# Six expert pairs' outputs go through DRAM and are fetched by token, in place of one-hot products

## The chip, the core and the metric

The kernel runs on one core of a Trainium2 chip. The metric is the device time of one execution in microseconds (us). TensorE (PE) does the matrix products and transposes, VectorE (DVE) and ScalarE (ACT) the elementwise work, GpSimd (POOL) broadcasts, fills and some DMA issues, and SyncE (SP) issues the weight loads.

## What is computed

A trunk of two layers on 256 tokens of 1024 values, fp32. In each layer three kinds of token mixer share one projection, then comes a layer norm, then a mixture of 16 experts of which every token uses two, chosen by a router within one of four groups, and a second layer norm. The part that the change touches:

```python
combine = jnp.einsum('tk,tke->te', top_w, one_hot(top_idx, N_EXPERTS))
out = jnp.zeros_like(t)
for e in range(N_EXPERTS):
    act = jax.nn.silu(t @ w_gate[e]) * (t @ w_up[e])
    out = out + combine[:, e:e + 1] * (act @ w_down[e])
...
h = layer_norm(DN_ALPHA * h + ffn, ln_ffn_g[layer], ln_ffn_b[layer])
```

The gate and up matrices are 1024 x 512 and the down matrix is 512 x 1024 for each expert.

## The kernel before

**Tiles.** Tokens stand in two tiles of 128 rows. Each expert has 64 slots (CAP); the tokens that chose it are gathered into them by one-hot products. A token beyond the 64th of an expert would be handled in a branch (`overflow`, L1400), which the given inputs don't enter. The experts are worked in eight pairs, each pair filling 128 slots.

**One pair p.** Gate: eight k-steps of two products each (one for each expert of the pair, 64 columns of weights to 512). Up: eight more. ACT takes Silu of the gate sums, DVE multiplies by the up sums. `by_slot` transposes the weighted one-hot matrix (two transposes into `sT`; `ws` is each slot's combine weight). `turn` transposes the activation (four transposes `aT`), which ACT copies to `actT`. Down: eight steps of two products into two banks `y`. ACT and DVE scale these by `ws` and split them into a high and a low part, `yt`. `scatter` of pair p then goes back to tokens: eight one-hot products `sc` (two token tiles, two halves of the columns, high and low part), whose sums DVE adds into `z`. It stands one pair later in PE's order, around `turn` of pair p+1, so that PE does not wait for the split. The scatter of pair 6 stands in pair 7's gate steps (`SC_AT`); pair 7's own one is spread over the end of the stage. For pairs 2, 4 and 6 one gather (`gather_two`) serves the pair and the one after it.

**The residual.** `halve` keeps the layer input as two parts. `residual`, called four times among pair 6's up steps (one call for each tile and half of the columns), sums the parts, scales them with the norm's two vectors and adds them to `z`: four DVE operations a call. The vectors come by `lnvec`: a 4 KB load on POOL's queue (L355) and a broadcast on POOL (L356).

**Weights.** Everything is loaded once, in tiles of 512 KB, into a ring of 33 slots (`fp`, NFEED). `more()` issues the next tile on SP's queue (L331). It is called once for each tile that PE has used up, and each tile waits for the use that freed its slot. Some tiles go into spare buffers instead (`more_extra`, L314 and L319, the names `wx`). SP issues in order: a load that waits holds up those behind it.

**Order.** In the expert stage each engine runs its instructions in the order in which the code issues them. A planner (`Order`) sets the order of the mixer stages only.

Of the kernel before, what the change touches and what calls it, by code (L numbers as in the profile page):

```python
# [65 lines left out]
N_P0 = 512  # L66
SCRATCH = 2048
# [168 lines left out]
def trunk_kernel(ctx, tc, x, positions, w_in, gate_up, gate_bias, norm_gain, w_out, ln_mix_g, ln_mix_b,  # L236
# [5 lines left out]
    pp = ctx.enter_context(tc.tile_pool(name="pp", bufs=8, space=bass.MemoryType.PSUM))  # L242
    ctx.enter_context(tc.manual_schedule())
# [160 lines left out]
    pref = cp.tile([P, E], F32, name="pref")  # L404
    nc.gpsimd.iota(pref, pattern=[[-1, E]], base=E, channel_multiplier=0, allow_small_or_imprecise_dtypes=True)
# [7 lines left out]
    rc = cp.tile([P, NT, 16], F32, name="rc")  # L413
    rs = cp.tile([P, NT, 2, 8], F32, name="rs")

    def trig_tables():
# [44 lines left out]
        for i in range(2):  # L461
            dve.tensor_copy(rc[:, :, 8 * i:8 * i + 8], trig4[:, 1])
# [53 lines left out]
    def rope(y, off, nh, t):  # L516
# [4 lines left out]
        dve.tensor_mul(ra, v[:, :, 0:16], rc[:, t, None, :].to_broadcast([P, nh, 16]))  # L521
# [197 lines left out]
    for l in range(DEPTH):  # L719
# [646 lines left out]

        def by_slot(Gw):
# [115 lines left out]
        sb, sts = {}, []  # L1483

# [6 lines left out]

        for p in range(E // 2):
            gu = []
            if p == E // 2 - 1:
                Gw = weights(p)
            for nm in ("g", "u"):
                b_ = bank("gu")
                for k in range(KT):
                    if k % 2 == 0:
                        us = [feed.pop((l, nm, p, k + e)) for e in range(2)]  # L1500
                    for e in range(2):
                        mm(b_[64 * e:64 * e + 64], xs[p](k, e), part(us[e], k % 2), start=k == 0, stop=k == KT - 1)
                        if k % 2 and type(us[e]) is not list:
                            more()
# [144 lines left out]
```

## Time and profile before

| | us |
|---|---|
| median of three runs | 746.43 (746.12 to 746.93) |
| the profiled execution | 745.53 |
| its span in the trace | 743.8 |
| PE busy | 715.8 (96%) |
| DVE busy | 373.4 (50%) |
| ACT busy | 255.0 (34%) |
| POOL busy | 43.4 (6%) |
| mean DMA rate over the span | 327 GB/s |

The span is the time from the first to the last recorded event; 1.7 us of the execution lie around it. A busy share is a mean over stages. The expert stage of layer 0 lies at about 155 to 366 us, that of layer 1 at about 515 to 733 us, and what bounds each is read from the stretch itself. In the timelines a line is a run of like instructions, with its start, its length, and in brackets what ended the idle time ahead of it. A product of fp32 is recorded as two instructions, so that x32 there are 16 products.

### The profile page before, as it was taken

What the parts mean: (1) busy time and instruction counts of PE and PEld (TensorE: products, weight loads), DVE (VectorE), ACT (ScalarE), POOL (GpSimd) and SP (SyncE); (2) the same over time, 40 slices, a digit from 0 to 9 for tenths busy, and PEclk for the clock granted to TensorE, in tenths of its full rate; (3) what the DMA queues carried; (4) which work ended last, traced back from release to release, by engine and by line L of the source; (5) the groups of instructions that cost most, each with busy time, mean ns of one, the idle gap of its engine ahead of it and who ended that gap; (6) DMA issues with size and microseconds to landing.
All of it is one profiled execution on the core that took longest, in us unless ns stands there. A gap on an engine that the chain in (4) does not pass through costs nothing. (4 is left out here: it accounts for less than half of the span.)

```text
span 743.8 us, 11218 instructions
## 1 busy us (share of the span) xinstructions
PE 715.8 (96%) x3941; PEld 419.2 (56%) x3941; DVE 373.4 (50%) x986; ACT 255.0 (34%) x527; POOL 43.4 (6%) x67
## 2 busy tenths in 40 slices
PE   7999999999999999999899999999999999999993
PEld 6897977754533533433388888777435344353331
DVE  5887866632312322561488688666231223336405
ACT  5667655422211201210186665563222111111101
POOL 2000001100000002200130000001000000020002
PEclk9999999999999999999999999999999999999997
DMA  8899836889999999999999654569898999999941
GB/s 299 281 392 408 322 135 214 325 312 371 364 343 410 408 410 408 408 409 400 332 387 351 221 176 143 195 207 360 316 380 334 367 408 409 409 408 408 406 177 56
DMA packets 81519, 243.04 MB, mean 327 GB/s; under 512 B 9956, under 2 KB 14120, under 8 KB 81448
## 3 DMA queue, kind: packets, MB, share of 16 engines
q1 hardware_dynamic: 80776, 241.86, 86.2%
q8 instruction: 36, 0.59, 0.3%
q10 hardware_dynamic: 416, 0.26, 0.1%
q14 instruction: 35, 0.29, 0.1%
q0 software_dynamic: 256, 0.03, 0.0%
HBM read 241.08 MB, written 1.05 MB: 326 GB/s over the span
## 5 line engine op out<-in xcount | busy, mean ns | idle before, releaser
L231 PE MATMUL gu<-wf,xT 128*64 128x512 f32 x944 | 224.3, 593 | 3.0 <-PEq L1400 3.0
L231 PEld LDWEIGHTS gu<-wf,xT 128*64 128x64 f32 x944 | 72.8, 137 | 136.8 <-issue 126.9
L231 DVE TENSOR_TENSOR wlo<-wf,whi 128x512 fp32r<-128x512 f32 (+2 forms) x174 | 97.3, 598 | 39.6 <-ACT whi L231 36.9
L231 PE MATMUL y<-wf,actT 128*64 128x512 f32 x456 | 110.7, 596 | 1.4 <-ACT actT L231 1.4
L231 ACT ACTIVATE whi<-wf 128x512 fp32r<-128x512 f32 (+2 forms) x176 | 86.8, 552 | 14.5 <-PE po L231 9.5
L231 DVE TENSOR_TENSOR act<-act,gu 128x512 f32<-128x512 f32 x16 | 11.0, 687 | 141.9 <-PE gu L231 86.5
L231 PE MATMUL pj<-whi,hhi 128*128 128x512 f32 (+2 forms) x224 | 81.7, 365 | 0.0
L231 PE MATMUL pj<-wlo,hhi 128*128 128x512 f32 (+2 forms) x224 | 78.2, 349 | 1.6 <-DVE wlo L231 1.5
L231 PE MATMUL pj<-whi,hlo 128*128 128x512 f32 (+2 forms) x224 | 77.7, 347 | 0.0
L231 DVE SCALAR_TENSOR_TENSOR yt<-y,ws,yt 128x512 fp32r<-128x512 f32 x32 | 23.8, 750 | 106.6 <-ACT yt L231 105.4
L231 PEld LDWEIGHTS y<-wf,actT 128*64 128x64 f32 x456 | 33.8, 137 | 58.5 <-issue 51.8
L231 ACT ACTIVATE yt<-y,ws 128x512 fp32r<-128x512 f32 x32 | 21.8, 688 | 100.6 <-PE y L231 100.1
L231 PEld LDWEIGHTS pj<-whi,hhi 128*128 128x128 f32 x224 | 42.1, 188 | 8.3 <-issue 2.9
L231 PEld LDWEIGHTS pj<-wlo,hhi 128*128 128x128 f32 x224 | 42.2, 188 | 7.1 <-DVE wlo L231 3.4
L231 PEld LDWEIGHTS pj<-whi,hlo 128*128 128x128 f32 x224 | 42.1, 188 | 5.2
L231 ACT ACTIVATE xT<-xT,cols 128x256 f32<-128x256 f32 (+1 forms) x40 | 18.2, 518 | 72.0 <-PE xT L231 72.0
L231 PE MATMUL sc<-yt,sT 128*128 128x512 f32 x128 | 36.7, 414 | 1.8 <-ACT yt L231 1.7
L231 ACT ACTIVATE act<-gu 128x512 f32<-128x512 f32 x16 | 9.6, 597 | 79.5 <-PE gu L231 67.0
L231 PE MATMUL gu<-wx,xT 128*64 128x512 f32 x80 | 36.6, 592 | 0.0
L231 ACT ACTIVATE actT<-aT 128x512 f32<-128x512 f32 x16 | 9.6, 598 | 70.0 <-PE aT L231 70.0
L231 DVE TENSOR_TENSOR z<-z,sc 128x512 f32<-128x512 f32 x48 | 29.7, 679 | 7.7 <-PE sc L231 7.7
L231 PEld LDWEIGHTS sc<-yt,sT 128*128 128x128 f32 x128 | 21.9, 189 | 12.5 <-issue 4.9
(269 smaller groups left out, 966.1 us busy)
## 6 DMA issues: line engine op xcount, KB each, us to landing
wf<-in_w_expert_up_dram SPq DMA_DIRECT2D x120, 512.0 KB, 9.6
wf<-in_w_expert_gate_dram SPq DMA_DIRECT2D x116, 512.0 KB, 7.6
wf<-in_w_expert_down_dram SPq DMA_DIRECT2D x114, 512.0 KB, 10.1
wf<-in_w_in_dram SPq DMA_DIRECT2D x32, 512.0 KB, 9.8
wf<-in_w_out_dram SPq DMA_DIRECT2D x16, 512.0 KB, 10.3
wx<-in_w_expert_down_dram SPq DMA_DIRECT2D x24, 256.0 KB, 6.0
wf<-in_w_in_dram SPq DMA_DIRECT2D x16, 292.0 KB, 5.9
wf<-in_w_in_dram SPq DMA_DIRECT2D x16, 264.0 KB, 4.9
```

The lines of the kernel that those rows point to most:

```text
L231: return fn(*a, **kw)
```

## The change

Pairs 0 to 5 (N_AWAY = 6) no longer scatter. Their down sums are scaled by `ws` into one tile `yw` (ACT one half, DVE the other), and a DMA on ACT's queue stores its 128 rows, 512 KB, in a DRAM buffer `away` of 768 rows. `yw` takes a slot of the weight ring. `rows_of` works out for each token, in eight small DVE operations, the rows of its two expert outputs in `away`; a row outside of the buffer (an expert of pairs 6 or 7, or a token beyond its expert's slots) is skipped. After pair 5, POOL clears `z` and `zb` (two tiles of 128 x 1024 each) and, at the second gate step of pair 6 in the code, `fetch` issues four indirect DMAs of 128 rows, one row for each token: first choices into `z`, second ones into `zb`. `residual` has one more addition, that of `zb`. `shares` gets `ws` from two products of two columns, where `by_slot` made two transposes. `scatter` remains for pairs 6 and 7.

Where PE's order had scatters ahead of the down products, gate steps of the next pair now stand (FILL: two ahead of `turn` and one behind it, or one behind it where a `gather_two` is there already). `yw` and `zb` take eight slots of the ring in each layer, and for these no `more()` is called. A smaller edit makes the table `rc` of the rotary embedding half as wide.

```diff
+N_AWAY = 6
+FILL = (2, 3)
+FETCH = (6, 1)
...
+            dve.tensor_add(r, zb[t][:, c], r)
             dve.tensor_add(z[t][:, c], z[t][:, c], r)
...
+        def shares(p):
+            b_ = bank("ws")
+            for t in range(NT):
+                mm(b_[:, 0:2], Gs[p][:, t].rearrange("p a b -> p (a b)"), comb[:, t * E + 2 * p:t * E + 2 * p + 2],
+                   start=t == 0, stop=t == NT - 1)
+            ws = sm("ws", 1)
+            for e in range(2):
+                dve.tensor_copy(ws[64 * e:64 * e + 64], b_[64 * e:64 * e + 64, e:e + 1])
+            od.free(b_)
+            return ws
+        def rows_of():
+            code, c2, rows = sm("code", 32), sm("code", 32), sm("rows", 2 * NT, I32)
+            code3, low = code.rearrange("p (t e) -> p t e", t=NT), sm("low", 2 * NT)
+            dve.tensor_scalar(code, pos, float(CAP), 4096.0, op0=OP.is_ge, op1=OP.mult)
+            dve.tensor_add(code, code, pos)
+            dve.tensor_add(code3, code3, first[:, None, :].to_broadcast([P, NT, E]))
+            dve.tensor_reduce(low[:, 0:NT], code3, AX.X, OP.min)
+            c3 = c2.rearrange("p (t e) -> p t e", t=NT)
+            dve.tensor_tensor(c3, code3, low[:, 0:NT, None].to_broadcast([P, NT, E]), op=OP.is_equal)
+            dve.scalar_tensor_tensor(c2, c2, 8192.0, code, op0=OP.mult, op1=OP.add)
+            dve.tensor_reduce(low[:, NT:2 * NT], c3, AX.X, OP.min)
+            dve.tensor_copy(rows, low)
+            return rows
...
         def scatter(p, yt, sT, tiles=range(NT)):
-            if p == 0:
-                z.extend(t4("z", (P, D)) for _ in range(NT))
             for t in tiles:
                 for n in range(2):
                     b_ = bank("sc")
                     place(b_, t, n, yt, sT)
                     zs = z[t][:, 512 * n:512 * n + 512]
-                    if p == 0:
-                        act.activation(zs, b_, AF.Copy)
-                    else:
-                        dve.tensor_add(zs, zs, b_)
+                    dve.tensor_add(zs, zs, b_)
                     od.free(b_)
+        def fetch():
+            for i, zt in enumerate(z + zb):
+                nc.gpsimd.indirect_dma_start(out=zt, out_offset=None, in_=away,
+                                             in_offset=bass.IndirectOffsetOnAxis(ap=rows[:, i:i + 1], axis=0),
+                                             bounds_check=N_AWAY * P - 1, oob_is_err=False)
...
+        rows = rows_of()
+        away = dp.tile([N_AWAY * P, D], F32, name="away", tag=f"away{l}")
+        zb = []
...
+        def step(p, nm, b_, k):
+            if k % 2 == 0:
+                us[nm] = [feed.pop((l, nm, p, k + e)) for e in range(2)]
+            for e in range(2):
+                mm(b_[64 * e:64 * e + 64], xs[p](k, e), part(us[nm][e], k % 2), start=k == 0, stop=k == KT - 1)
+                if k % 2 and type(us[nm][e]) is not list:
+                    more()
+            if (p, nm) == (FIN, "u") and k in BEGIN:
+                begin(*((0, 0), (1, 0), (0, 1))[BEGIN.index(k)])
+            if (p, nm, k) == (FIN, "g", SC_AT):
+                scatter(*late)
+            if (p, nm, k) == (FIN, "g", OVER_AT):
+                overflow()
+            if nm == "g" and (p, k) == FETCH:
+                fetch()
+            if k % 2 and (p, nm) in AT:
+                {"h": halve, "r": residual}[AT[p, nm]](k // 4, k // 2 % 2)
+        def gate(p, upto):
+            if p not in gates:
+                gates[p], done_k[p] = bank("gu"), 0
+            while done_k[p] < upto:
+                step(p, "g", gates[p], done_k[p])
+                done_k[p] += 1
...
+            if p < N_AWAY:
+                ws = shares(p)
+            else:
+                sT, ws = by_slot(Gw)
...
-            elif p + 1 in xs:
-                scatter(*late, (0,))
+            elif p == 0:
+                gather(1, G, turn)
+            else:
+                if p + 1 in TWO:
+                    gather_two(p + 1, G)
+                else:
+                    gate(p + 1, FILL[0])
                 turn()
-                scatter(*late, (1,))
-            elif not late:
-                gather(p + 1, G, turn)
-            else:
-                (gather_two if p + 1 in TWO else gather)(p + 1, G)
-                turn()
-                scatter(*late)
+                gate(p + 1, FILL[1] if p + 1 not in TWO else FILL[1] - FILL[0])
...
+                        elif p < N_AWAY and yw is None:
+                            yw = fp.tile([P, D], F32, name="yw", tag="wf")
+                        elif p == N_AWAY - 1 and len(zb) < NT:
+                            zb.append(fp.tile([P, D], F32, name="zb", tag="wf"))
...
-                    split(py[n], *yt[n], scale=ws)
-                if p == E // 2 - 1:
+                    if p < N_AWAY:
+                        c = slice(512 * n, 512 * n + 512)
+                        if n == 0:
+                            act.activation(yw[:, c], py[n], AF.Copy, scale=ws)
+                        else:
+                            dve.tensor_scalar(yw[:, c], py[n], ws, None, op0=OP.mult)
+                            nc.scalar.dma_start(away[p * P:(p + 1) * P], yw)
+                    else:
+                        yt[n] = [t2("yt", dt=F32R) for _ in range(2)]
+                        split(py[n], *yt[n], scale=ws)
+                if final:
...
+            if p >= N_AWAY:
+                late = p, yt, sT
+            if p == N_AWAY - 1:
+                z.extend(t4("z", (P, D)) for _ in range(NT))
+                for zt in z + zb:
+                    pool.memset(zt, 0.0)
```

**PE, layer 0, from pair 5's `turn` to the scatter of pair 6.** `gu` are gate and up sums, `sc` scatters, `y` down sums, `aT` and `sT` transposes. Before:

```order
L231 MATMUL aT<-ident,act 128x128 x4
L231 MATMUL sc<-yt,sT 128x512 x8
L231 MATMUL y<-wf,actT 64x512 x16
L231 MATMUL gu<-wf,xT 64x512 x32
L231 MATMUL sT<-ident,Gw 128x128 x2
L231 MATMUL sc<-yt,sT 128x512 x4
L231 MATMUL aT<-ident,act 128x128 x4
L231 MATMUL sc<-yt,sT 128x512 x4
L231 MATMUL y<-wf,actT 64x512 x16
L231 MATMUL gu<-wf,xT 64x512 x12
L231 MATMUL sc<-yt,sT 128x512 x8
```

And now:

```order
L234 MATMUL aT<-ident,act 128x128 x4
L234 MATMUL gu<-wf,xT 64x512 x2
L234 MATMUL y<-wf,actT 64x512 x16
L234 MATMUL gu<-wf,xT 64x512 x30
L234 MATMUL sT<-ident,Gw 128x128 x2
L234 MATMUL gu<-wf,xT 64x512 x4
L234 MATMUL aT<-ident,act 128x128 x4
L234 MATMUL gu<-wf,xT 64x512 x2
L234 MATMUL y<-wf,actT 64x512 x16
L234 MATMUL gu<-wf,xT 64x512 x6
L234 MATMUL sc<-yt,sT 128x512 x8
```

The scatters of pairs 4 and 5 are gone; one gate step of pair 6 (x2) and three of pair 7 (x4 and x2) have moved ahead of the down products in their places. The scatter of pair 6 remains.

**POOL, layer 0, from the last vector's broadcast on.** `mc` are constants of the next mixer. Before:

```order
L355 DMA vec<-in_ln_ffn_b_dram 1x16x64
L356 ISA vec<-vec 128x1024
L375 MEMSET mc 128x256
L376 AFFINE_SELECT mc<-mc 128x128
L378 AFFINE_SELECT mc<-ones 128x128
```

And now:

```order
L360 ISA vec<-vec 128x1024
L234 MEMSET z 128x1024 x2
L234 MEMSET zb 128x1024 x2
L1429 DMA z<-away,rows 128x1024 x2
L1429 DMA zb<-away,rows 128x1024 x2
L379 MEMSET mc 128x256
L380 AFFINE_SELECT mc<-mc 128x128
L382 AFFINE_SELECT mc<-ones 128x128
```

Four clears and four fetches stand between the broadcast and the next layer's constants.

**SP, layer 1, from the last loads into spare buffers to the load of a counter `cnti`.** Before:

```order
L314 DMA wx<-in_w_expert_up_dram 128x1024
L314 DMA wx<-in_w_expert_down_dram 128x1024
L314 DMA wx<-in_w_expert_gate_dram 128x1024
L331 DMA wf<-in_w_expert_down_dram 128x1024 x4
L331 DMA wf<-in_w_expert_gate_dram 128x1024 x6
L331 DMA wf<-in_w_expert_up_dram 128x1024 x7
L331 DMA wf<-in_w_expert_down_dram 128x1024 x3
L1580 TENSOR_LOAD cnti
```

And now:

```order
L318 DMA wx<-in_w_expert_up_dram 128x1024
L318 DMA wx<-in_w_expert_down_dram 128x1024
L318 DMA wx<-in_w_expert_gate_dram 128x1024
L335 DMA wf<-in_w_expert_up_dram 128x1024 x7
L335 DMA wf<-in_w_expert_down_dram 128x1024 x5
L335 DMA wf<-in_w_expert_gate_dram 128x1024 x6
L335 DMA wf<-in_w_expert_up_dram 128x1024
L1653 TENSOR_LOAD cnti
```

The tiles that follow the last spare load belong to an earlier place in the weights than before; behind it SP has eight more tiles ahead of any given one.

## Rows read from the trace of the kernel before

**Rows 1.** The page: span, engines, groups (line, operation, tiles, count, busy, mean ns, idle).

```profile
span 743.8 us, 11218 instructions
...
PE 715.8 (96%) x3941; PEld 419.2 (56%) x3941; DVE 373.4 (50%) x986; ACT 255.0 (34%) x527; POOL 43.4 (6%) x67
...
L231 PE MATMUL gu<-wf,xT 128*64 128x512 f32 x944 | 224.3, 593 | 3.0 <-PEq L1400 3.0
...
L231 PE MATMUL y<-wf,actT 128*64 128x512 f32 x456 | 110.7, 596 | 1.4 <-ACT actT L231 1.4
...
L231 ACT ACTIVATE actT<-aT 128x512 f32<-128x512 f32 x16 | 9.6, 598 | 70.0 <-PE aT L231 70.0
```

**Rows 2.** Busy by stretch: length, PE, PEld, DVE, ACT, POOL, clock, DMA share, GB/s.

```profile
155.00:225.00 70.00, 70.00 (x364) 31.14 (x364) 19.03 (x49) 16.29 (x31) 0.00 (x0) 1.00 0.91 345
...
225.00:350.00 125.00, 123.52 (x600) 50.96 (x596) 44.67 (x82) 16.32 (x27) 9.10 (x13) 1.00 1.03 408
...
515.00:600.00 85.00, 83.91 (x442) 38.11 (x442) 25.59 (x79) 19.37 (x35) 0.00 (x0) 1.00 0.94 354
...
600.00:717.00 117.00, 115.48 (x560) 48.08 (x556) 41.17 (x74) 14.94 (x25) 7.32 (x8) 1.00 1.01 400
```

**Rows 3.** Timeline of SP's queue: start, us, issues.

```profile
310.90 9.30 SPq L331 DMA_DIRECT2D wf<-in_w_expert_gate_dram  x8
...
341.61 7.98 SPq L331 DMA_DIRECT2D wf<-in_w_in_dram  x7
...
514.43 0.33 SPq L314 DMA_DIRECT2D wx<-in_w_expert_gate_dram  x1
...
676.55 9.13 SPq L331 DMA_DIRECT2D wf<-in_w_expert_gate_dram  x8
```

**Rows 4.** DMA issues (230 to 320; last: whole span), median us to landing.

```profile
wf<-in_w_expert_gate_dram SPq DMA_DIRECT2D x26, 512.0 KB, 10.2
...
vec<-in_ln_ffn_b_dram POOLq DMA_DIRECT2D x1, 4.0 KB, 5.4
...
out_dram<-z SPq DMA_DIRECT2D x3, 256.0 KB, 2.0
```

**Rows 5.** Timeline of PE, layer 0: pairs 5 to 7, next mixer's first product.

```profile
300.60 2.09 PE L231 MATMUL sc<-yt,sT 128*128 128x512 f32 x8
...
302.62 7.09 PE L231 MATMUL y<-wf,actT 128*64 128x512 f32 x32
...
309.54 13.90 PE L231 MATMUL gu<-wf,xT 128*64 128x512 f32 x64
...
323.37 0.44 PE L231 MATMUL sT<-ident,Gw 128*128 128x128 f32 x2
...
324.58 0.60 PE L231 MATMUL aT<-ident,act 128*128 128x128 f32 x4
...
326.04 7.09 PE L231 MATMUL y<-wf,actT 128*64 128x512 f32 x32
...
372.19 1.15 PE L231 MATMUL pj<-wf,hT 128*128 128x292 f32 x4
```

**Rows 6.** The same of layer 1: pair 6's down products.

```profile
691.12 7.09 PE L231 MATMUL y<-wf,actT 128*64 128x512 f32 x32
```

**Rows 7.** Timeline of POOL: fourth vector's transfer and broadcast, layer 0.

```profile
306.61 0.51 POOL L355 DMA_DIRECT2D vec<-in_ln_ffn_b_dram  x1 [6.11 <-PE y L231]
...
312.13 1.29 POOL L356 PARTITION_BROADCAST vec<-vec  x1 [5.02 <-DMA vec<-in_ln_ffn_b_dram]
```

**Rows 8.** POOL's instructions by line: a clear of 128x1024.

```profile
L231 POOL MEMSET aM<- 128x1024 f32 x2 | 1.9, 958 | 130.3 <-PE pT L231 66.4 <-DVE acc L231 64.0
```

**Rows 9.** Timeline of DVE: last addition of a quarter, product of gate and up.

```profile
317.44 0.69 DVE L231 TENSOR_TENSOR z<-z,whole 128x512 f32<-128x512 f32 x1
...
323.61 0.68 DVE L231 TENSOR_TENSOR act<-act,gu 128x512 f32<-128x512 f32 x1
```

**Rows 10.** Busy by stretch, after PE's last product (columns of Rows 2).

```profile
736.00:744.00 8.00, 0.00 (x0) 0.00 (x0) 4.53 (x5) 0.35 (x1) 2.61 (x2) 0.51 0.35 131
```

More of the change, by code (lines that the diff above doesn't have):

```diff
@@ L403, in trunk_kernel @@
     nc.gpsimd.iota(iota, pattern=[[1, CAP]], base=0, channel_multiplier=0, allow_small_or_imprecise_dtypes=True)
-    pref = cp.tile([P, E], F32, name="pref")
-    nc.gpsimd.iota(pref, pattern=[[-1, E]], base=E, channel_multiplier=0, allow_small_or_imprecise_dtypes=True)
+    pref = cp.tile([P, 4], F32, name="pref")
+    nc.gpsimd.iota(pref, pattern=[[-1, 4]], base=E, channel_multiplier=0, allow_small_or_imprecise_dtypes=True)
+    first = cp.tile([P, E], F32, name="first")
+    nc.gpsimd.iota(first, pattern=[[CAP, E]], base=0, channel_multiplier=0, allow_small_or_imprecise_dtypes=True)
     below = cp.tile([P, 4, 4], I32, name="below")
@@ L460, in trig_tables @@
         trig4 = trig.rearrange("p (s t j) -> p s t j", s=2, t=NT)
-        for i in range(2):
-            dve.tensor_copy(rc[:, :, 8 * i:8 * i + 8], trig4[:, 1])
+        dve.tensor_copy(rc, trig4[:, 1])
         dve.tensor_scalar(rs[:, :, 0], trig4[:, 0], -1.0, None, op0=OP.mult)
@@ L1492, in trunk_kernel @@
+        def gate(p, upto):
[4 more added lines that the diff above has]
+                done_k[p] += 1
         for p in range(E // 2):
-            gu = []
-            if p == E // 2 - 1:
+            final = p == FIN
+            if final:
                 Gw = weights(p)
[L1496 to L1504, printed above, removed]
-                    if (p, nm) == (E // 2 - 1, "u") and k in BEGIN:
-                        begin(*((0, 0), (1, 0), (0, 1))[BEGIN.index(k)])
-                    if (p, nm, k) == (E // 2 - 1, "g", SC_AT):
-                        scatter(*late)
-                    if (p, nm, k) == (E // 2 - 1, "g", OVER_AT):
-                        overflow()
-                    if k % 2 and (p, nm) in AT:
-                        {"h": halve, "r": residual}[AT[p, nm]](k // 4, k // 2 % 2)
-                gu.append(b_)
-                if nm == "g":
-                    av = t2("act")
-                    act.activation(av, b_, AF.Silu)
-                    if p + 1 < E // 2:
-                        Gw = weights(p)
-                        if p + 1 not in Gs:
-                            G = slots(p + 1)
@@ L1521, in trunk_kernel @@
-            dve.tensor_mul(av, av, gu[1])
-            od.free(*gu)
-            sT, ws = by_slot(Gw)
+            gate(p, KT)
+            av = t2("act")
+            act.activation(av, gates[p], AF.Silu)
+            if not final:
+                if p >= N_AWAY:
+                    Gw = weights(p)
+                if p + 1 not in Gs:
+                    G = slots(p + 1)
+            bu = bank("gu")
+            for k in range(KT):
+                step(p, "u", bu, k)
+            dve.tensor_mul(av, av, bu)
@@ L1551, in trunk_kernel @@
             yt = [None, None]
-            us = [feed.pop((l, "d", p, i)) for i in range(8)]
-            final = p == E // 2 - 1
+            ud = [feed.pop((l, "d", p, i)) for i in range(8)]
+            yw = None
             for i in range(8):
```

21 lines of the change are left out of this document (12 added, 9 removed).

## The prediction

> **What bounds the kernel now.** I read the page's head and its costly groups first [rows 1]: TensorE (PE) is busy for 715.8 of 743.8 us, and its two large groups in the expert stage waited for nothing that costs: 3.0 us before gate and up products (that is the overflow branch), 1.4 before down products. By that alone, work taken off PE is time won. Next I read the busy times by stretch [rows 2], since a share over the whole span hides stages. In the first part of each expert stage PE never idles and the DMA engines move 345 and 354 GB/s; in the second part PE is still full, but DMA is full too, at 408 and 400 GB/s. So the stage is bounded twice there. How near the second bound lies is read from SyncE's (SP) weight issues [rows 3] and their time to landing [rows 4] against PE's order [rows 5]. The eight gate tiles of pair 7 are issued from 310.90 on, and a full DMA passes one in 1.28 us (512 KB at 408 GB/s). The second is out at 312.2 and down 10.2 later, at 322.4. PE reads it after pair 6's down products, at 326.04 + 6.9 = 333. Ten us of lead: whatever PE wins beyond that, or DMA gets to carry beside it, is a wait for weights.
>
> **What comes off PE.** Each scatter is eight products, 2.02 us from start to next start [rows 5]. Five stood before the end of pair 5's down products: 10.1. Of the two 128-wide transposes per pair (0.44 together [rows 5]) two-column products remain; I credit a quarter, 0.1 a pair, 0.5. That is 10.6 per layer, and 12.7 for all six pairs. One gate step of pair 6 (13.9/16 = 0.87) now runs earlier, ahead of pair 5's down products. Pair 5 ended at 302.62 + 7.09 = 309.7; less 10.6, plus 0.87, it ends at **T = 300.0**. The other 15 steps of pair 6 take 13.0, so PE asks for pair 7's first gate step at 313.2, since three such steps now stand ahead of pair 6's down products, in the place of the scatter. Its second tile lands at 322.4 even with nothing added. The early steps thus pull PE's wait forward; the wait itself is set by DMA.
>
> **What is added to DMA.** Six stores of 512 KB, 3.15 MB, at 408 GB/s [rows 2]: 7.7 us a layer. Four fetches of 128 rows of 4 KB; if the router spreads tokens evenly, 12 of 16 experts are away, so 3/4 of the rows move: 1.57 MB, 3.9 us. Together 11.6 us of traffic a layer. Some of it fits into idle time of the first part: 70 us at 345 instead of 408 GB/s leave 10.8 us in layer 0, 85 at 354 leave 11.3 in layer 1 [rows 2]. SP issues a tile only when PE has freed its slot, so not all of that can be taken. In layer 0 I take 5: the first two stores (2.6) fit, and PE frees slots a little earlier. In layer 1 the order is changed too: the rows that become stores and zb take ring slots, and behind the last spare-buffer load (514.43 [rows 3]) SP stands 8 weight tiles further back than before, 8 x 1.28 = 10.3 us. With slots waiting for SP the queue has no more gaps, so there I take 10 of 11.3.
>
> The Trainium skill, *DMA: Bandwidth & Descriptors*, "Issuing engines are not separate DMA queues", says that transfers started by any engine run on the same 16 DMA engines and interleave; it speaks against this change, since a store put on ScalarE's (ACT) queue would still cost the loads its 1.28 us. No run here shows a store beside loads. If it fails, the sum loses 7.7 a layer and becomes rival B.
>
> Layer 0: 322.4 + 11.6 - 5 = 329.0. Steps 0 and 1 and the transposes of 0.60 run meanwhile; step 2's two tiles come 2.6 after the second, and it takes 0.87: pair 6's down products start at 332.5, against 326.04 [rows 5]. Three steps are already done then, 3 x 0.87 = 2.6: **+3.9**. Layer 1: 676.55 + 1.26 + 10.2 + 11.6 + 10.3 - 10 = 699.9 [rows 3]; down products 3.5 after it, 703.4, against 691.12 [rows 6], less 2.6: **+9.7**. Pair 7's down tiles are later by no more than that and had some 8 us of lead; they don't bind again.
>
> **The fetch.** GpSimd (POOL) now clears four tiles and then fetches, and only then can the residual add zb. POOL's last vector broadcast ended at 312.13 + 1.29 = T + 3.7 [rows 7]; four clears of 0.96 [rows 8] make T + 7.5. The fetch also waits for pair 5's store: 2.0 us for the one store with no load beside it, 10.2 for a load in the full queue [rows 4], so T + 2 to T + 10.2. Say T + 9; an issue is 0.51 [rows 7], so the third fetch goes out at +1.5, and a 4 KB transfer of POOL's queue took 5.4 to land [rows 4]: zb's first tile is there at T + a with **a = 16**. Bounds: 7.5 + 1.0 + 2.0 = 10 with nothing in the way; 10.2 + 1.5 + 10.2 + 3.9 = 26 if each fetch queues as a load does. By the figure of the same page, "Anatomy of one DMA — SWDGE (gpsimd) path" (2.0 us plus the bytes), I estimate 2.9 a fetch, so a near 11.6; the row at 5.4 for only 4 KB disagrees, and it decides.
>
> Behind zb stand on VectorE (DVE), in order: two adds (1.3), three further quarters of the residual, five operations of 0.69 each [rows 9], 10.4, and the product of gate and up (0.68), for which the transposes (0.60), their copy (0.60 [rows 1]) and the down products wait: with 0.3 between, 13.9. Down products at T + a + 13.9 = 329.9 for a = 16. The stage shifts by 300.0 + a + 13.9 - 326.04 - 2.6 = a - 14.7, here +1.3: hidden under the weights' +3.9 and +9.7. The bound is thus the later of two chains, not their sum.
>
> **Edits costed at nothing.** The index arithmetic: eight DVE operations on 32 columns, below 8 x 0.69 = 5.5 a layer if each cost as much as 512 columns and nothing covered it; DVE stands idle half the time, gate products of pair 0 cover it. The store stands on ACT's queue behind DVE's half of the row block (about 0.7), and nothing is queued behind it there until the next gate's Silu, several us later. POOL's fetches hold up the next layer's constants, read 60 us later. The next mixer's weights: first issue 341.61 [rows 3], first product 372.19 [rows 5], 30.6 less 10.2 leaves 20 us; even 8 late is covered.
>
> **The clock.** After PE's last product the granted clock stood at 0.51 [rows 10], half of 2.4 GHz; in the stage it was 1.00 [rows 2]. A wait of 10 us or more on PE may bring it down, and the products after it then take twice as long; three steps at half cost 2.6 more, none costs 0. I take 1 a layer.
>
> **Sum (A):** 3.9 + 9.7 + 2 = 15.6. The profiled execution took 745.5 (span 743.8): 761.1. The median of the runs, 746.43, is 0.9 above it: **762.0**. Unknowns: idle time recovered (5 of 10.8, 10 of 11.3: +-5 each), the clock (0 to 5).
>
> **Rivals.** *B, stores cost loads nothing* (reads and writes pass each other): 7.7 less a layer, so the weights give -3.8 and +2.0, the fetch chain +1.3 in each: 1.3 + 2.0 + 2 = 5.3, 751.7. For it: no row has a store beside loads; against it: 16 engines at 1.03 of their time. *C, faster:* the whole traffic finds gaps, and the fetch lands at a = 10; layer 0 goes by the fetch, -4.7 (weights 3.9 - 11.6 = -7.7), layer 1 by the weights, 9.7 - 11.6 = -1.9; no clock loss: 739.8. It decides once a is under 14.7 and less than about half of the traffic delays loads. The far end is PE alone, 2 x -12.7: 721; it would need weights ten us ahead of their issue. *D, slow fetch:* a = 26 gives +11.3 a layer, above the weights, plus 2: 771.0. For it: rows gathered one by one by POOL, of which no row here tells a price. *No change:* B with an early fetch, or the gain and the delay meet.
>
> **How the numbers follow.** A 0.47, D 0.14, B 0.17, C 0.17, no change 0.05. What this kernel's measurement can tell from no change is about 0.2%, 1.5 us. Slower by more: A, D and most of B, 0.75; faster by more: C and the lucky edge of B, 0.19; within: 0.06. Range: 741 leaves out a little over half of C (0.10), 781 the tail of D (a above 28, or A with nothing recovered and the clock at its worst), 0.06. Cases slower than before hold most of the chance; A's own range is 754 to 770.
>
> **What would show it.** PE's wait before the gate steps at pair 6's transposes, with a weight load as releaser: about 329.0 - 313.2 = 16 us in layer 0 and more in layer 1, and DMA at 400 GB/s or more through it. If DVE's add of zb ends the wait instead, the fetch is the bound (a read from the first to the last gather). If the gate products' rows show no wait and scatters are gone, C. A store that lands in 2 us beside loads speaks for B. The forecast is wrong if loads keep their 10.2 us and spacing of 1.28 with stores between them.

## The result, and the profile after

The changed kernel takes 792.77 us (median, 792.27 to 795.4), the kernel before, measured beside it, 746.27 us: a ratio of 1.063, 95% interval 1.0605 to 1.0657. That is 46 us slower, beyond the end of the range (781). The direction was forecast; the size was three times too small. The execution that was profiled was the slowest of the four, 795.4 us.

The page after. To be read against [rows 1]: PE is as busy as before (718.6 against 715.8 us) though 96 scatter products are gone, and gate and up products now idle for 38.3 us, 32.5 of them for gate weights and 5.8 at the overflow branch. DVE waits 40.2 us for `zb`, in two waits.

```profile
span 793.7 us, 11005 instructions
...
PE 718.6 (91%) x3869; PEld 416.7 (53%) x3869; DVE 338.3 (43%) x933; ACT 243.1 (31%) x507; POOL 59.0 (7%) x84
...
L234 PE MATMUL gu<-wf,xT 128*64 128x512 f32 x944 | 245.8, 618 | 38.3 <-DMA wf<-in_w_expert_gate_dram 32.5
...
L234 DVE TENSOR_TENSOR whole<-zb,whole 128x512 f32<-128x512 f32 x8 | 5.5, 692 | 40.4 <-DMA zb<-away,rows 40.2
```

PE's timeline of the changed kernel, layer 0, from the end of pair 6's up products (start, us; in brackets the idle time ahead and what ended it). It answers to [rows 5], where down products stood at 326.04:

```profile
319.42 0.44 PE L234 MATMUL sT<-ident,Gw 128*128 128x128 f32 x2
333.10 4.15 PE L234 MATMUL gu<-wf,xT 128*64 128x512 f32 x8 [13.25 <-DMA wf<-in_w_expert_gate_dram]
343.77 1.11 PE L234 MATMUL aT<-ident,act 128*128 128x128 f32 x4 [6.51 <-DVE act L234]
344.81 1.98 PE L234 MATMUL gu<-wf,xT 128*64 128x512 f32 x4
346.57 8.66 PE L234 MATMUL y<-wf,actT 128*64 128x512 f32 x32
...
362.54 1.94 PE L234 MATMUL gu<-wf,xT 128*64 128x512 f32 x6 [2.70 <-PEq L1436]
```

PE stands twice: 13.25 us at the gate steps that were pulled ahead, for weights, and then 6.51 us at the transposes, for DVE's product of gate and up. Down products start at 346.57, 20.5 later. In layer 1, where they stood at 691.12 [rows 6] and the stage starts 22.5 later, PE stands twice as well, and DVE waits for `zb`:

```profile
726.46 4.95 PE L234 MATMUL gu<-wf,xT 128*64 128x512 f32 x8 [12.11 <-DMA wf<-in_w_expert_gate_dram]
736.03 1.11 PE L234 MATMUL aT<-ident,act 128*128 128x128 f32 x4 [4.62 <-DVE act L234]
...
738.84 7.09 PE L234 MATMUL y<-wf,actT 128*64 128x512 f32 x32
```

```profile
723.44 0.69 DVE L234 TENSOR_TENSOR whole<-zb,whole 128x512 f32<-128x512 f32 x1 [18.98 <-DMA zb<-away,rows]
```

Why DVE was late is told by three queues. The store of pair 5 on ACT's queue, the clears and fetches on POOL's, DVE's first addition of `zb` and its product, all of layer 0:

```profile
311.31 0.33 ACTq L1631 DMA_DIRECT2D away<-yw  x1
```

```profile
301.57 1.95 POOL L234 MEMSET zb<- 128x1024 f32 x2
318.88 1.14 POOL L1429 DMA_INDIRECT z<-away,rows  x1 [15.36 <-DMA wf<-in_w_expert_down_dram]
...
321.63 0.99 POOL L1429 DMA_INDIRECT zb<-away,rows  x1 [0.30 <-issue]
```

```profile
309.27 0.69 DVE L234 SCALAR_TENSOR_TENSOR whole<-vec,whole 128x512 f32<-128x512 f32 x1
331.18 0.69 DVE L234 TENSOR_TENSOR whole<-zb,whole 128x512 f32<-128x512 f32 x1 [21.21 <-DMA zb<-away,rows]
...
343.03 0.68 DVE L234 TENSOR_TENSOR act<-act,gu 128x512 f32<-128x512 f32 x1
```

Pair 5's down products end at 306.6. The store goes out at 311.31, POOL can fetch at 318.88 (the row names a load that landed then; in the program POOL waits for the stores and its own clears), the third fetch leaves at 321.63, and `zb` is there at 331.18, 24.6 us after pair 5. From there it is 15.4 to the down products.

DMA issues of the whole span (KB each, median us to landing), to be read against [rows 4]. The trace has the landing of one store only; in e6 below, where it has all twelve, they took 6.8 to 8.1:

```profile
away<-yw ACTq DMA_DIRECT2D x12, 512.0 KB, 7.3
...
z<-away,rows POOLq DMA_INDIRECT x4, 8.8
zb<-away,rows POOLq DMA_INDIRECT x4, 10.9
```

And the stretches (columns of [rows 2]). The first part of layer 0's stage still moves 345 GB/s, now with two stores in it. While PE stands, the granted clock goes to 0.50 of 2.4 GHz, and it is at 0.52 when PE works again. In layer 1 DMA falls to 334 GB/s from 20 to 40 us after the stage's first gate product; before, it moved 382 there:

```profile
155.00:225.00 70.00, 70.00 (x370) 30.92 (x368) 15.09 (x46) 12.87 (x24) 0.00 (x0) 1.00 0.91 345
...
325.00:330.00 5.00, 0.00 (x0) 0.00 (x0) 0.00 (x0) 0.00 (x0) 0.31 (x2) 0.50 1.03 404
345.00:350.00 5.00, 5.00 (x14) 1.38 (x14) 0.00 (x0) 0.52 (x1) 0.00 (x0) 0.52 1.03 408
563.00:583.00 20.00, 20.00 (x97) 6.64 (x91) 4.53 (x10) 3.58 (x6) 0.00 (x0) 1.00 0.87 334
```

### The profile page after: what moved, and what is told of

It reads as the page before. It is cut to its first block, busy times and chain, and to the rows that moved or that the text cites. A ratio compares the mean times of both kernels' runs of the same rounds, so it can differ in the third digit from the quotient of the medians.

```text
span 793.7 us, 11005 instructions
## 1 busy us (share of the span) xinstructions
PE 718.6 (91%) x3869; PEld 416.7 (53%) x3869; DVE 338.3 (43%) x933; ACT 243.1 (31%) x507; POOL 59.0 (7%) x84
## 5 line engine op out<-in xcount | busy, mean ns | idle before, releaser
L234 PE MATMUL gu<-wf,xT 128*64 128x512 f32 x944 | 245.8, 618 | 38.3 <-DMA wf<-in_w_expert_gate_dram 32.5
L234 PEld LDWEIGHTS gu<-wf,xT 128*64 128x64 f32 x944 | 78.4, 141 | 170.9 <-issue 125.4
L234 PE MATMUL y<-wf,actT 128*64 128x512 f32 x456 | 115.0, 606 | 1.5 <-ACT actT L234 1.5
L234 ACT ACTIVATE whi<-wf 128x512 fp32r<-128x512 f32 (+2 forms) x176 | 86.7, 552 | 13.9 <-PE po L234 9.6
L234 PEld LDWEIGHTS y<-wf,actT 128*64 128x64 f32 x456 | 37.8, 141 | 62.4 <-issue 53.1
L234 DVE TENSOR_SCALAR yw<-y,ws 128x512 f32<-128x512 f32 x12 | 9.0, 751 | 106.9 <-PE y L234 83.5
L234 ACT ACTIVATE yw<-y,ws 128x512 f32<-128x512 f32 x12 | 8.2, 687 | 86.2 <-PE y L234 79.8
L234 DVE TENSOR_SCALAR xT<-xT,cols 128x256 f32<-128x256 f32 (+1 forms) x40 | 17.4, 485 | 28.5 <-PE xT L234 22.5
L234 DVE TENSOR_TENSOR whole<-zb,whole 128x512 f32<-128x512 f32 x8 | 5.5, 692 | 40.4 <-DMA zb<-away,rows 40.2
## 6 DMA issues: line engine op xcount, KB each, us to landing
wf<-in_w_expert_up_dram SPq DMA_DIRECT2D x120, 512.0 KB, 10.1
wf<-in_w_expert_down_dram SPq DMA_DIRECT2D x114, 512.0 KB, 10.2
```

What stands on the lines that cost most here:

```text
L234: return fn(*a, **kw)
```

## The experiments

The theories, drawn from the changed kernel's trace: **W**, weights come late because of the added bytes; **F**, the chain of store, fetch and DVE's additions holds pair 6's down products; **L**, eight tiles fewer are issued ahead in layer 1. Two more came from the runs: **K** (later **S**), SP stands behind stores, and **X**, the early gate steps make PE wait.

All runs, with the length of the expert stage from its first gate product to the end of pair 7's last down product, as the difference to the kernel before (209.7 us in each layer: 155.58 to 365.3 and 520.66 to 730.4). These lengths are of the profiled executions, one of each kernel:

| kernel | median us | layer 0 | layer 1 |
|---|---|---|---|
| changed kernel | 792.8 | +21.1 | +27.1 |
| e1, no store, no fetch | 751.4 | +2.9 | +1.0 |
| e2, stores, no fetch | 771.6 | +9.3 | +16.9 |
| e3, residual in pair 7 | 777.1 | +11.6 | +19.5 |
| e4, no early gate steps | 786.8 | +18.4 | +18.0 |
| e5, eight tiles issued again | 788.0 | +20.4 | +21.1 |
| e6, stores on POOL's queue | 785.2 | +17.0 | +20.5 |
| e7, e3, e5 and e6 at once | 772.1 | +12.7 | +14.5 |
| e8, e1 without early gate steps | 747.9 | 0.0 | -0.1 |
| e9, two pairs away | 746.7 | +0.3 | -0.2 |
| e10, rows outside of the ring | 782.5 | +18.1 | +17.4 |
| e11, two pairs, outside of the ring | 740.9 | -0.7 | -3.2 |
| e12, e10 with a quarter of each row | 766.9 | +10.4 | +10.1 |

The runs of before beside them had medians of 745.87 to 746.48.

**e1.** The store and the call of `fetch` are left out:

```diff
-                            nc.scalar.dma_start(away[p * P:(p + 1) * P], yw)
...
-            if nm == "g" and (p, k) == FETCH:
-                fetch()
```

> The changed kernel without its stores and without its four fetches (six pairs' outputs are left out of the sum, so the output is not the reference's); everything else stands: scatters gone, gate steps pulled ahead, eight ring slots taken per layer. Theory F (the fetch decides: store of pair 5, fetch, DVE's additions of zb, then pair 6's down products): no wait of DVE for zb is left; pair 6's down products of layer 0 start at about 326 in place of 346.6, and the whole falls from 792.8 to about 746. Theory W (weights come late because of the added traffic): the wait before pair 7's first gate step falls from 13.25 us to 1 to 3 in layer 0, and the whole comes to about 746 too. Theory L (the weights are late because eight tiles fewer are issued ahead, whatever the traffic): the wait before the gate steps stays above 8 us in layer 1, and the whole stays above 755.

Measured: 751.4. DVE has no wait for `zb`, layer 1 does not stay high, so L, as the whole cause, falls. But the kernel is still 5 us slower than before (ratio 1.006, 1.0037 to 1.0083), without a byte of added traffic and without 12 scatters. Its waits, in PE's table (us in total, times, longest), and its first stretch:

```profile
PE gu L234 <- DMA wf<-in_w_expert_gate_dram: 9.4, 2, 4.9
```

```profile
155.00:225.00 70.00, 70.00 (x369) 30.27 (x369) 15.07 (x46) 13.36 (x25) 0.00 (x0) 1.00 0.92 346
```

So with nothing added, PE already runs into the weights at pair 7's first gate step, 4.9 us in layer 0. That wait isn't what makes the stage longer: pair 6's down products start 1.9 us later in the stage than before, but three gate steps of pair 7 (2.6) are done by then. The 2.9 us come behind them, at the overflow branch:

```profile
343.26 7.07 PE L234 MATMUL gu<-wf,xT 128*64 128x512 f32 x24 [3.29 <-PEq L1436]
```

Before, PE waited 1.48 there, and the 24 gate products took 5.37; now the granted clock behind the branch is 0.66 in the mean from 344 to 349, where it was 1.00. That is 1.8 and 1.7, less the 0.7 of lead.

**e2.** Only the call of `fetch` is left out.

> The changed kernel with its stores but without its four fetches (six pairs' outputs are left out of the sum, so the output is not the reference's). Theory F: DVE's wait for zb is gone and pair 6's down products start when the weights allow it, 333.1 - 3.9 + 3.5 = about 332.7 in layer 0 instead of 346.6; the whole is about 762, some 30 us less than the changed kernel. Theory W: the fetch moved only 3.9 us of data a layer, so the whole falls by no more than 8, to about 785.

Measured: 771.6, between the two. Twelve stores cost 20.2 us over e1, where their bytes come to 12 x 1.28 = 15.4. In layer 0 they cost 6.4, less than the 7.7 of their bytes; in layer 1 they cost 15.9. There SP's timeline has a hole between the up and the down tiles of a pair:

```profile
545.20 9.45 SPq L335 DMA_DIRECT2D wf<-in_w_expert_up_dram  x7
563.52 3.15 SPq L335 DMA_DIRECT2D wf<-in_w_expert_down_dram  x5
```

**e3.** The residual's calls, with the additions of `zb`, are moved from pair 6's up steps into pair 7's gate steps:

```diff
-AT = {(1, 'g'): 'h', (6, 'u'): 'r'}
+AT = {(1, 'g'): 'h', (7, 'g'): 'r'}
```

> Complete kernel; the residual's four calls, which wait for zb on DVE, move from pair 6's up steps to pair 7's gate steps, so that the product of gate and up of pair 6 no longer stands behind them. Same stores, same fetch. Theory F: pair 6's down products start at 333.1 + 3.5 = 336.6 in layer 0, 10 us earlier than in the changed kernel, about 9 earlier in layer 1, unless the wait comes back where pair 7 needs z: about 773. Theory W: the first gate step of pair 7 sets the end, whatever DVE waits for, and the whole stays within 3 us of 792.8.

Measured: 777.1, 15.7 less than the changed kernel. In PE's timeline the wait for weights stays and the wait for DVE is gone:

```profile
332.44 4.24 PE L234 MATMUL gu<-wf,xT 128*64 128x512 f32 x8 [13.45 <-DMA wf<-in_w_expert_gate_dram]
336.61 0.65 PE L234 MATMUL aT<-ident,act 128*128 128x128 f32 x4
```

F holds for what lies above the weights, 9.6 and 7.6 us in the two layers; W for the rest. The chain of the fetch was the later one of the two.

**e5.** Eight more `more()` calls behind layer 0:

```diff
-        more(2)
+        more(10)
         h = z
```

> Complete kernel; after the expert stage of layer 0 eight more weight tiles are issued ahead, which the stored tiles had kept back in the ring, so that layer 1 starts with as many tiles ahead as before. Theory L: layer 1's waits for gate tiles (1.95, 4.18 and 12.11 us) lose 8 x 1.28 = 10 us, and the whole falls by about 10, to 783. Theory F: the fetch sets the end of layer 1; only what lies ahead of pair 5's store comes back, about 6 us, to 787.

Measured: 788.0, as F said. Layer 1 gains 6.0; its two smaller waits for gate tiles (1.95 and 4.18) go, and the fetch sets the end.

**e6.** The stores go out by `nc.gpsimd.dma_start`.

> Complete kernel; the stores go out by GpSimd's queue in place of ScalarE's, the same bytes. In the program the loads of SP and the DMAs of ACT share eight completion counters in turn, so a weight load waits until the DMA eight places ahead of it in the program has landed, a store among them; GpSimd's DMAs have counters of their own. Theory K (SP stands behind late stores): SP's 25 us of waits for stores in layer 1 are gone, the DMA rate of layer 1's first 100 us has no hole any more, and the whole falls by about 8, to 785. Rival (a store costs its bytes and nothing else): within 2 us of 792.8.

Measured: 785.2, the figure of K. SP's waits for stores fell by half, not to nothing:

```profile
SPq L335 <- DMA away<-yw: 15.5, 4, 6.2
```

In the changed kernel that row reads:

```profile
SPq L335 <- DMA away<-yw: 34.7, 7, 10.4
```

The expectation named the shared completion counters only. What remains is another link, which the program's order with its waits shows. This is SP around the turn from pair 0 to pair 1 of layer 0 in the changed kernel:

```
L335 DMA wf<-in_w_expert_gate_dram 128x1024 [waits DMAHW4_49,PE_49]
L335 DMA wf<-in_w_expert_gate_dram 128x1024 [waits DMAHW5_49,DMAHW6_49,DVE_49,Activation_49]
L335 DMA wf<-in_w_expert_gate_dram 128x1024 [waits PE_49]
```

Before, the loads at this place wait for one counter and for PE. The second one here waits for DVE, ACT and two counters: it has the ring slot in which `yw` stood, and one of the two counters is the store's. That load is the seventh that SP issues behind the store, not the first, as e10's expectation has it; it must wait until the store has landed, and SP's queue waits with it. In e6, where stores have counters of their own, the same load still waits for the store, for DVE and for ACT, by the slot alone. The counters bind in the other direction too: in the changed kernel pair 5's store waits for the load eight places ahead of it, and goes out at 311.31; in e6 it goes out at 305.63.

**e7.** The edits of e3, e5 and e6 together.

> Complete kernel with three edits at once: stores on GpSimd's queue, residual in pair 7's gate steps, eight more tiles issued ahead behind layer 0. If the three causes (DVE's wait for zb 15.7, missing tiles 4.8, SP behind stores 8) add up: 792.8 - 28 = about 764. If they hide each other, no lower than 772. What is left above 746 is then the bytes themselves and what the early gate steps do.

Measured: 772.1, so they do hide each other: 20.6 below the changed kernel, and 20.7 above e1. The second figure is what e7 has and e1 has not. Most of it is bytes, 2 x 11.6 = 23.2 by the prediction's own sum; but SP still waits 11.3 us for stores in e7, so bytes and waits aren't parted there.

**e8.** e1, and FILL = (0, 0): nothing stands where the scatters stood.

> As e1 (no store, no fetch, six pairs' outputs left out of the sum), and also without the gate steps that were put ahead of the down products. Theory X (the early gate steps make pair 6's down products wait for weights that are only on their way): without them pair 6's down products start at about 318 in place of 328.3 in layer 0, the loads run on beside them, and the stage ends when the last down tiles land, some 8 us a layer earlier: about 735. Rival (the weights' arrival sets the end whatever PE's order): 748 to 751, as e1.

Measured: 747.9 (ratio 1.0014, 0.9999 to 1.003), close to the rival's figure, but not for its reason: in e8 PE has no wait for a weight tile in the expert stages. Both stages have the length of before within 0.1 us. Part of the reason is in the rows of pair 4, first of the kernel before and then of e8, from the end of the up products to the down products:

```profile
272.70 0.44 PE L231 MATMUL sT<-ident,Gw 128*128 128x128 f32 x2
...
275.37 3.22 PE L231 MATMUL y<-wf,actT 128*64 128x512 f32 x13
```

```profile
272.07 0.61 PE L234 MATMUL ws<-comb,G 128*128 128x2 f32 x4
273.02 0.66 PE L234 MATMUL aT<-ident,act 128*128 128x128 f32 x4 [0.34 <-DVE act L234]
274.36 3.22 PE L234 MATMUL y<-wf,actT 128*64 128x512 f32 x14 [0.69 <-ACT actT L234]
```

2.67 us with a scatter, 2.29 without: eight products of 2.02 us were worth 0.38. They had covered DVE's product (0.34) and ACT's copy (0.69), and the two-column products cost more than the transposes. At pair 5, where a gather stands ahead of `turn`, a scatter is worth 0.82 by the same count. Together that is a gain: pair 5's down products start 144.1 us after the stage's first gate product, before 147.0. Pair 6 loses it again:

```profile
324.03 0.66 PE L234 MATMUL aT<-ident,act 128*128 128x128 f32 x4 [2.05 <-DVE act L234]
325.37 8.78 PE L234 MATMUL y<-wf,actT 128*64 128x512 f32 x32 [0.69 <-ACT actT L234]
```

```profile
325.00:330.00 5.00, 4.63 (x14) 1.44 (x16) 0.00 (x0) 0.32 (x1) 0.00 (x0) 0.66 1.03 407
```

PE waits 2.05 for DVE's product, which stands behind the residual's twenty operations (sixteen before), and behind the two waits the granted clock is 0.66 in the mean, before 1.00: the down products take 8.78 in place of 7.09. So 2.9 us were gained and 2.9 lost. That the stage came out as long as before is a coincidence, and neither theory is what happened.

**e4.** The changed kernel with FILL = (0, 0).

> The changed kernel, complete, without the gate steps that were put ahead of the down products where scatters stood (FILL 0). Theory F: pair 6's down products wait for DVE's product behind the additions of zb either way, so the end moves by less than 5 us: 788 to 797. Theory X (PE stands at pair 7's early gate steps for 13 us and loses its clock by that): pair 6's down products no longer stand behind gate tiles, PE doesn't lose its clock, and the whole falls by 8 or more, to 785 or less.

Measured: 786.8, between the two, so X is not settled by it. PE then stands 21.34 us at one place in layer 0 in place of 13.25 and 6.51 at two, for DVE behind `zb`:

```profile
342.16 1.11 PE L234 MATMUL aT<-ident,act 128*128 128x128 f32 x4 [21.34 <-DVE act L234]
```

**e10.** Six pairs, rows outside of the ring (the edit also puts the stores on POOL's queue):

```diff
-                            yw = fp.tile([P, D], F32, name="yw", tag="wf")
...
+                        yw = t2("yw")
                         if n == 0:
-                            act.activation(yw[:, c], py[n], AF.Copy, scale=ws)
+                            act.activation(yw, py[n], AF.Copy, scale=ws)
                         else:
-                            dve.tensor_scalar(yw[:, c], py[n], ws, None, op0=OP.mult)
-                            nc.scalar.dma_start(away[p * P:(p + 1) * P], yw)
+                            dve.tensor_scalar(yw, py[n], ws, None, op0=OP.mult)
+                        nc.gpsimd.dma_start(away[p * P:(p + 1) * P, c], yw)
...
-        more(2)
+        more(4)
         h = z
```

> Complete kernel, six pairs through DRAM as in the changed kernel, residual where it was, but the rows to be stored stand in two spare buffers of 512 columns in place of a slot of the weight ring, each stored at once by GpSimd's queue; only zb's two slots are taken from the ring, and two tiles are issued again behind layer 0. In the changed kernel the first weight tile that SP issues behind a pair gets the slot that the stored rows leave, so SP waits for the store to land. Theory S (that wait on SP, with the tiles not issued, is the cause of the loss in layer 1): SP has no wait for a store any more, PE's waits for gate tiles of pairs 4 and 5 are gone, and the whole falls to 774 to 778, 8 to 10 below the kernel with GpSimd's stores alone (785.2). Rival (bytes and DVE's wait for zb are all that is left): 783 to 786.

Measured: 782.5, half a us under the rival's range. SP has no wait for a store any more and PE none ahead of pair 7, but only 2.7 us come of it over e6: with six pairs, bytes and DVE's wait for `zb` cover that cost.

**e12.** As e10, with 256 columns of each row (`away` is 256 wide; the stores and the fetches' targets are cut to it).

> As the kernel with its rows outside of the ring, but only 256 of the 1024 columns of each row are stored and fetched (three quarters of six pairs' outputs are left out of the sum, so the output is not the reference's): the traffic falls from 11.6 to 2.9 us a layer, with as many fetches and half as many stores. Theory bytes: 8.7 us a layer less, and the fetch lands earlier too: 17 to 24 below the kernel with whole rows. Rival (the number of fetches and their wait in the queue counts, not the bytes): within 6 of it.

Measured: 766.9, 15.5 less than e10; by stage 7.7 and 7.3, where 8.7 of bytes were taken away. That is near the theory's 17 and far from the rival's 6. The fetches land sooner with fewer bytes:

```profile
z<-away,rows POOLq DMA_INDIRECT x4, 5.7
zb<-away,rows POOLq DMA_INDIRECT x4, 5.8
```

**e9 and e11.** Two pairs away in place of six. e9, against the changed kernel:

```diff
-N_AWAY = 6
-FETCH = (6, 1)
+N_AWAY = 2
+FETCH = (2, 1)
...
-            dve.tensor_add(r, zb[t][:, c], r)
...
                                              bounds_check=N_AWAY * P - 1, oob_is_err=False)
+            for t in range(NT):
+                pool.tensor_add(z[t], z[t], zb[t])
...
+                elif late:
+                    scatter(*late, (0,))
                 else:
                     gate(p + 1, FILL[0])
                 turn()
+                if late:
+                    scatter(*late, range(NT) if p + 1 in TWO else (1,))
+                else:
+                    gate(p + 1, FILL[1] if p + 1 not in TWO else FILL[1] - FILL[0])
...
-                            nc.scalar.dma_start(away[p * P:(p + 1) * P], yw)
+                            nc.gpsimd.dma_start(away[p * P:(p + 1) * P], yw)
```

`rows_of` stands behind pair 0, `ws` comes by transposes as before, and `more(2)` behind the layer is `more(6)`. e11 is e9 with e10's edit on `yw` (two halves outside of the ring, and `more(4)`).

> Complete kernel, another mix: only pairs 0 and 1 go through DRAM (stores on GpSimd's queue, while DMA has gaps), the fetch is in pair 2, GpSimd adds zb into z, the index arithmetic stands behind pair 0's gate and up, the slot weights come by transposes as before, four tiles are issued again behind layer 0, and pairs 2 to 7 scatter by products. PE loses two scatters a layer, 4 us; the traffic is 2 x 1.3 + 1.3 = 3.9 us a layer, of which DMA's gaps take some. Expected if PE bounds and the loads keep their lead: 740. Rival (the loads' lead is what counts, as in e1): 746 or a little above.

> Complete kernel; as the one with pairs 0 and 1 through DRAM (746.7), but the stored rows stand in two spare buffers outside of the ring, so that SP doesn't wait for stores between 180 and 220 us. Theory S: DMA moves more than 345 GB/s in the first part of the stage, PE's lead at pair 7 grows by some 5 us, the half clock behind the branch goes, and the whole comes to about 743. Rival (two scatters less are worth nothing while loads bound the stage): 746 to 747.

Measured: e9 746.7, no change (ratio 1.0, 0.9988 to 1.0012), and e11 740.9, 0.7% faster than the kernel before (0.9933, 0.9915 to 0.9951). Between the two lies mainly where the stored rows stand; e11 also stores them in halves and issues two tiles fewer behind the layer. SP's waits from 150 to 230 us, in e9:

```profile
SPq L335 <- DMA away<-yw: 9.0, 2, 4.8
```

In e11 that row is missing, and the first part of layer 0's stage moves more than [rows 2] had, stores included:

```profile
155.00:225.00 70.00, 70.00 (x366) 29.87 (x367) 17.06 (x50) 13.36 (x25) 10.23 (x12) 1.00 0.94 353
```

In both kernels and both layers the two scatters less bring pair 6's down products 3.4 us forward (167.0 us after the stage's first gate product, before 170.5). What is kept of that is decided in pair 7. Its first 24 gate products of layer 1, in e9 and then in e11:

```profile
697.01 3.07 PE L234 MATMUL gu<-wf,xT 128*64 128x512 f32 x10
700.31 2.34 PE L234 MATMUL gu<-wf,xT 128*64 128x512 f32 x8 [0.22 <-DMA wf<-in_w_expert_gate_dram]
702.85 1.93 PE L234 MATMUL gu<-wf,xT 128*64 128x512 f32 x6 [0.20 <-DMA wf<-in_w_expert_gate_dram]
```

```profile
694.51 5.32 PE L234 MATMUL gu<-wf,xT 128*64 128x512 f32 x24
...
703.61 5.37 PE L234 MATMUL gu<-wf,xT 128*64 128x512 f32 x24 [1.75 <-PEq L1438]
```

In e9 they take 7.8 us, since the tiles come late, in e11 5.3. With the branch (2.24 and 1.75) that is 2.9 of the 3.0 between the two stages; behind the branch both keep their clock in this layer. So here the loads' lead counts, as e9's rival and e11's theory had it. In layer 0 e11 keeps only 0.7 of its 3.4: the branch takes 2.38 and the 24 products behind it 7.07, with the clock at 0.57 from 341 to 345. The half clock that was to go is still there.

## Why the prediction was wrong

The frame held: PE's saving is not worth what it seems because weights bound the second part, and the end is set by the later of two chains. The step that failed is "here +1.3: hidden under the weights' +3.9 and +9.7". The fetch was put at a = 16 behind pair 5's end; it came at 24.6 and, in layer 1, at 22.3, and pair 5 ended later than was credited, so the chain that was to be hidden is the one that set the end. The weights' chain was sized too small besides. By the steps:

1. **What comes off PE: mis-sized.** 10.6 us were credited up to pair 5. Counted from the stage's first gate product, pair 5's down products start 6.3 us earlier in e1, with one gate step (0.87) done ahead of them, so 7.2 came off. With nothing in the scatters' places it was 2.9 (e8), since they had covered the way from DVE's product to `actT`. With the early gate steps as cover, a pair takes 23.9 us (e1, starts of down products from pair 1 to pair 5) against 25.3 before, 1.5 less and not 2.1. The credit for two-column products had the wrong sign: the 0.44 that was read is the length of two transposes, the next start comes after 0.20; in e1 the two-column products take 0.54 to the next start (268.78 to 269.32). Pair 5's down products ended at 306.6 in layer 0, not at 300.0; 1.4 of that is a later start of the whole stage.

2. **Weights: right in kind, the recovery failed.** PE was to find its gate tile at 329.0; it found it at 333.1, or 331.7 without the stage's later start. The step that failed is "In layer 0 I take 5" of the idle DMA time: with none recovered the sum gave 322.4 + 11.6 = 334.0, so some 2 were. In layer 1, where 10 were taken, DMA's mean over the first 80 us rose from 354 to 369 GB/s, 3 us of traffic. The bytes themselves were sized well: 20.7 between e1 and e7 against 23.2 (with the waits that e7 still has), and 15.5 for three quarters of them (e12). As to the sentence of the Trainium skill, *DMA: Bandwidth & Descriptors*, "Issuing engines are not separate DMA queues", the runs agree: six stores on ACT's queue cost 6.4 us in layer 0, near the 7.7 of their bytes, and 15.9 in layer 1, where SP waited for them too (e2 over e1). Rival B falls with it.

3. **The fetch: a = 16 failed; it was 24.6, near rival D's 26.** Of its terms, POOL could fetch 12.3 after pair 5 and not 9: the clears were long done (303.5), but the store went out only at 311.31, 3.9 us after its rows were written, and took about 7.5. The third issue came 2.75 later and not 1.5. The fetch took 9.6 from its third issue to DVE's addition and not 5.4. The row chosen for it, 4 KB on POOL's queue, was nearest in queue and far in bytes; the 10.2 of a load was the better neighbour. The estimate from the Trainium skill, *DMA: Bandwidth & Descriptors*, "Anatomy of one DMA — SWDGE (gpsimd) path", was 2.9 us a fetch; beside the loads 8.8 and 10.9 were measured, and 5.7 for a quarter of the bytes, so the measurement decides. The a of 11.6 that was drawn from it doesn't follow from the terms beside it either: 9 + 1.5 + 2.9 is 13.4.

4. **Two chains, the later one counts: right, and D decided.** By e3 the fetch lay 9.6 and 7.6 above the weights. Rival D's own sum, with the sizes measured, accounts for layer 0: 11.3 (a = 26), less 1.4 (a was 24.6), plus 5.2 (pair 5 late by 6.6, of which 1.4 the start), plus 1.5 (15.4 behind `zb`, not 13.9), plus 4.5 (below), 21.1, as measured. For layer 1 the prediction took pair 5's end from layer 0, 144.4 us after the stage's first gate product. It was 157.9: 3.3 are the smaller saving (e1), the other 10.2 waits for gate tiles ahead of the down products of pairs 4 and 5, with the half clock behind them. With a = 22.3 and 15.4 behind `zb`, down products start 25.2 later; less three steps, plus 1.6 at the branch and 2.8 behind it, that gives 27.0 of 27.1.

5. **The clock: 1 us a layer failed.** The 1 was a choice, and no row gave it. At 0.5 the first steps cost twice, and the clock fell again at the second wait. In layer 0 pair 6's down products took 8.66 in place of 7.09, the 24 gate products behind the branch 7.07 in place of 5.37, and the branch itself 2.70 in place of 1.48: together 4.5. Nor was a wait of 10 us needed: e8 ran at half clock behind waits of 2.05 and 0.69, e1 behind the branch's 3.29.

6. **"Edits costed at nothing": one was not.** The prediction asked what is queued behind the store on ACT, and found nothing. The queue that stood behind it was SP's, by the ring slot that `yw` left and by the shared counters: 34.7 us of SP's waits, 30.2 in layer 1, DMA at 334 GB/s there. With six pairs, stores on POOL's queue gave 7.6 (e6), though that also brought the fetch forward; with two pairs, mainly the place of the rows decided between no change and a gain (e9, e11).

7. **Layer 1's eight tiles: smaller than said.** 10.3 of loss less 10 of recovery stood in the sum. e5 gives 6.0 in layer 1 for issuing them again, with the fetch setting the end there.

Taken together: 46 us are 5.0 that are left without any traffic (e1, in the stages the branch and the half clock behind it), 20.7 that e7 has over e1, bytes for the most part, and 20.6 of waits that three edits take away: DVE behind `zb`, SP behind stores, and the missing tiles. These three overlap, and the runs don't part them to better than a few us. Open stays why PE's wait at the branch is 2.7 to 3.3 us in the kernels with early gate steps of pair 7, 2.3 and 2.2 in e9, 2.4 and 1.75 in e11, and 1.5 before, in e8 and in layer 1 of e4.

## What to carry to other kernels

Products that stand between an engine's result and its use may be cover: before counting them as saved, look at what waits at that place when they are gone. A stage that keeps its length may still hide a gain and a loss (e8), so compare it pair by pair. A transfer that leaves a buffer of a ring also delays whoever gets that buffer next, so rows that wait for a store belong outside of the ring that feeds the loads. And in these runs bytes cost least where the profile shows DMA with gaps: two pairs there, with their rows outside of the ring, gained 0.7%; six pairs, which reach into the full part, lost 6%.

## What the runs showed of the hardware that was not expected

Beside the full stream of loads a fetch by index took about as long to land as a load of 512 KB (10.2 [rows 4]): 8.8 and 10.9 us in the median for 128 rows of 4 KB, 5.7 for rows of 1 KB. An issue took 1.0 to 1.1 us of POOL, where 0.51 had been taken from a plain one. In PE's wait from 319.9 to 333.1 the granted clock was 0.50 between 325 and 330; once PE worked again, behind the second wait, it was still 0.52 over the stretch from 345 to 350.

The same code reached its first gate product in layer 0 either 4.1 or 5.6 us after its first gather product, from kernel to kernel; the stage lengths above are counted from the gate product for that reason. The granted clock tells the two apart: from 151 to 156 it was 0.66 in the mean in the changed kernel and e8, which took 5.6, and 1.00 before and in e1, which took 4.1. All six kernels with 5.6 (also e3, e5, e6 and e10) have such a stretch at half clock there, and none of the others has one. Why it falls in some of them is open.
